# Expert gates: one-hot rows built per token in f16, members spread over ten pairs, gates from pair 21

## The chip, the cores and the metric

The kernel runs on one core of a Trainium2 chip. The metric is device microseconds (us) from launch to the end of that core. The kernel before takes 1699.96 us, the median of three runs (1698.5 to 1701.6).

## The reference, cut to what matters

Two transformer-like blocks run over 256 tokens of width 1024. The change lies in the last layer of the second block, a layer of 16384 experts (128 x 128). Each of 8 heads picks 16 experts for a token, and their softmax gives 16 gates.

```python
s = jnp.einsum('thpd,hpnd->thpn', q, sub_keys)
sc, idx = lax.top_k(s, PEER_TOPK)
cand = (sc[:, :, 0, :, None] + sc[:, :, 1, None, :]).reshape(T, PEER_HEADS, PEER_TOPK * PEER_TOPK)
cidx = (idx[:, :, 0, :, None] * PEER_NKEYS + idx[:, :, 1, None, :]).reshape(...)
top_sc, pos = lax.top_k(cand, PEER_TOPK)
eidx = jnp.take_along_axis(cidx, pos, axis=-1)
gate = jax.nn.softmax(top_sc.astype(jnp.float32), axis=-1).astype(h.dtype)
act = jax.nn.gelu(jnp.einsum('thkd,td->thk', u_tab[eb], hb), approximate=False)
y = jnp.einsum('thk,thkd->td', gb * act, v_tab[eb])
```

## The kernel before, in words

All of the change is in `experts(hx)`. The kernel does not gather the chosen experts. It computes the activations of all 16384 for all tokens, multiplies them by a gate that is zero for those not chosen, and sums over all.

The loop `for m in range(KEYS // 2)` runs over 64 pairs of weight tiles (128 experts a tile). For each tile, `weights` loads 512 KB (`wraw`), ScalarE rounds it to a high part (`whi`, L99), VectorE or GpSimd subtracts that from the raw tile to get the low part (`wlo`, L100: GpSimd below pair 11, VectorE from there), and TensorE does 24 matmuls of 256 columns (`mm3`, L119 to L121: high by high, high by low, low by high, so that the third matmul of a tile is the first that needs `wlo`). There are three buffers of each of `wraw`, `whi` and `wlo`. ScalarE applies Gelu to a pair's result (L1370, L1372).

Beside the first pairs, VectorE chooses the experts. `choosing` is a generator whose steps the table `pace` deals out, so many before each pair: two steps of `keys_of`, four of `pairs` for each half of the tokens, and then `members`, which finds the two key numbers of every chosen expert: eight steps, four for each half of the tokens, in turn one of two VectorE instructions over 2048 elements (L1267, L1270) and one of a reduction over 2048 (L1272). Some of them are kept in program order. The rest is placed by a scheduler, within each engine's own queue.

At pair `DIRECT`, `softmaxes` makes two tables: `tab` (the two key numbers) and `gtab` (the gate in two f16 parts), with the chosen expert on the partition and the token along the row. From then on `gates(t4, n)` is called `PACE` times a pair on average, 64 times in all, for four tokens at a time. It builds one-hot rows: `oij` (is this row's key number equal to the column's number, for both key numbers), and `og` (the second one-hot times the gate, in two parts). Eight matmuls of 128 columns (L1326) multiply them to the 128 x 128 table of gates of each of the four tokens, and the result is multiplied into the activations by VectorE (L1329) or laid down ahead for the pairs to come by ScalarE (L1331). The tiles `oij` and `og` have two buffers each.

After the last pair, a second loop of 128 tiles sums the weighted rows (L1396); its first matmul waits for all gates.

Of the kernel before, what the change touches and what calls it, by code (L numbers as in the profile page):

```python
# [13 lines left out]
F16 = mybir.dt.float16  # L14
U32 = mybir.dt.uint32
AF = mybir.ActivationFunctionType
ALU = mybir.AluOpType
# [29 lines left out]
def two_blocks(ctx: ExitStack, tc: tile.TileContext, A, out):  # L47
    nc = tc.nc
    act, vec, pool, pe = nc.scalar, nc.vector, nc.gpsimd, nc.tensor
# [34 lines left out]
    def bank(name):  # L84
        ids = banks[-1][name]
        ids.append(ids.pop(0))
        return ps.tile([128, 512], F32, name=name, tag=f"bank{ids[-1]}")
# [96 lines left out]
    with psum(mm=8):  # L184
        o = bank("mm")
# [6 lines left out]
    for k in range(KC):  # L192
        if k % 4 < 2:
            first[k % 4] = next(loads[k % 4])
        t = hp.tile([128, T1], F32, name=f"h{k}")
# [932 lines left out]
    def experts(hx):  # L1128
        NEGL = -3.0e38

        GATE = 2.0 ** 14
        DIRECT = 18
        PACE = 1.5
        es = ExitStack()
        early = ExitStack()
        early.enter_context(psum(mm=6, sc=2))
# [11 lines left out]
        for i in range(2):  # L1148
            for e2 in range(2):
                o = bank("sc")  # L1150
                for k in range(4):
                    pe.transpose(o[:, k * 128:(k + 1) * 128], hx[4 * e2 + k][:, i * 128:(i + 1) * 128], ident)
                t = qp.tile([128, 2, S], F32, name="pair").rearrange("p a b -> p (a b)")
# [7 lines left out]
        for n in range(6):  # L1161
            o = bank("mm")
            project(o[:, :S + 2], wt(A["peer_wq"][n], vec if n == 1 else pool), raw, t1=S + 2)
            rp.append(o)
            if n == 0:
                o = bank("sc")
# [9 lines left out]
        p = es.enter_context(tc.tile_pool(name="ex", bufs=1))  # L1176
        iota = p.tile([128, 128], F32, name="iota")
        nc.sync.dma_start(out=iota, in_=A["iota"])
        acts = p.tile([128, KEYS, S], F32, name="acts")

        tab = p.tile([128, 2, S], F32, name="tab")
        gtab = p.tile([128, 2, S], F32, name="gtab")
# [92 lines left out]
        def expert_acts(m, e, pin):  # L1275

            o = bank("mm")
            for e2 in range(2):
                hi, lo = wt(A["peer_u"][2 * m + e2], e, pin=pin)
                for k in range(KC):  # L1280
                    c = slice(k * 128, (k + 1) * 128)
                    mm3(o[:, e2 * S:(e2 + 1) * S], hi[:, c], lo[:, c], u3[k][0], u3[k][1], k == 0, k == KC - 1)
            return o.rearrange("p (a b) -> p a b", a=2)
# [26 lines left out]
        def gates(t4, n):  # L1310

            o = bank("sc")
            ts = slice(4 * t4, 4 * t4 + 4)
            oij = pg.tile([128, 2, 4, 128], F16, name="oij")
            og = pg.tile([128, 2, 4, 128], F16, name="og")
            vec.tensor_tensor(out=oij, in0=iota[:, None, None, :].to_broadcast([128, 2, 4, 128]),  # L1316
                              in1=tab[:, :, ts][:, :, :, None].to_broadcast([128, 2, 4, 128]), op=ALU.is_equal)
            for part in range(2):
                if part and t4 % 2:
                    vec.tensor_mul(og[:, 1], oij[:, 1], gtab[:, 1, ts][:, :, None].to_broadcast([128, 4, 128]))  # L1320
                else:
                    for k in range(4):
                        act.activation(og[:, part, k], oij[:, 1, k], AF.Copy, scale=gtab[:, part, 4 * t4 + k:4 * t4 + k + 1])  # L1323
            for k in range(4):
                for part in range(2):
                    pe.matmul(o[:, k * 128:(k + 1) * 128], lhsT=og[:, part, k], rhs=oij[:, 0, k], start=part == 0, stop=part == 1)  # L1326
            gv = o.rearrange("p (n i) -> p i n", n=4)
            av = acts[:, :, ts]
            vec.tensor_mul(av[:, :n], av[:, :n], gv[:, :n])  # L1329
            if n < KEYS:  # L1330
                act.copy(av[:, n:], gv[:, n:])  # L1331
# [8 lines left out]
        def choosing():  # L1340

            for q in range(NH - 2, NH):
                yield from keys_of(q)
            for i in range(2):
                yield from pairs(i)
            for i in range(2):
                yield from members(i)
# [1 line left out]


        steps = choosing()
        pace = (1, 1, 1, 2, 1, 1, 1, 2, 1, 1, 0) + (1, 1, 1, 1, 1, 1, 0)
        OTHER = 11
        done = 0
        for m in range(KEYS // 2):
            if m < DIRECT:
                for n in range(pace[m]):
                    next(steps)
            if m == DIRECT:
                for _ in steps:  # L1360
                    pass
                softmaxes()
                et.close()
                eg = ExitStack()
                pg = eg.enter_context(tc.tile_pool(name="exg", bufs=2))
            o = expert_acts(m, pool if m < OTHER else vec, OTHER <= m < DIRECT)
            a = acts[:, 2 * m:2 * m + 2]
            if done:
                t = qp.tile([128, 2, S], F32, name="pair")
                act.activation(t[:, :, :done], o[:, :, :done], AF.Gelu)  # L1370
            if done < S:
                act.activation(a[:, :, done:], o[:, :, done:], AF.Gelu)  # L1372
            if done:
                vec.tensor_mul(a[:, :, :done], a[:, :, :done], t[:, :, :done])
            if m >= DIRECT:
                for _ in range(int((m - DIRECT + 1) * PACE) - int((m - DIRECT) * PACE)):
                    if done < S:
                        gates(done // 4, 2 * m + 2)
                        done += 4
# [28 lines left out]
        part = acts[:, 16:24].rearrange("p (i a) b -> p i (a b)", i=4)  # L1408
# [4 lines left out]
        for i in range(2):  # L1413
            for n in range(3):
                add(ws[n], i, False, n == 2)
            for e2 in range(2):
                fs = slice(e2 * 512, (e2 + 1) * 512)
                t, x = part[:, 2 * i + e2], hf[:, i, fs]
# [23 lines left out]
    gated_mix()  # L1442
    stages.close()
    experts(hx)


# [133 lines left out]
```

## Time and profile before

| what | value |
|---|---|
| runs, median of three | 1699.96 us |
| profiled execution, its own time | 1698.82 us |
| its span on the core | 1697.0 us |
| mean granted TensorE clock | 0.992 |
| PE busy | 1659.4 us, 98% |
| VectorE (DVE) busy | 1298.1 us, 76% |
| ScalarE (ACT) busy | 1011.0 us, 60% |

The span runs from the first to the last instruction of the core, and 1.8 us of the execution's own time lie around it. Busy shares are means over the whole span. Matmuls overlap, so a duration of 0.28 us in a row is longer than the distance from one start to the next, about 0.12 us for 256 columns. The same holds to a smaller degree on VectorE: an instruction starts about 0.08 us before the end of the one ahead of it. What an instruction costs its engine is the distance from its start to the next one's, which is called its pitch below.

### The profile page before, as it was taken

What the parts mean: (1) busy time and instruction counts of PE and PEld (TensorE: products, weight loads), DVE (VectorE), ACT (ScalarE), POOL (GpSimd) and SP (SyncE); (2) the same over time, 40 slices, a digit from 0 to 9 for tenths busy, and PEclk for the clock granted to TensorE, in tenths of its full rate; (3) what the DMA queues carried; (4) which work ended last, traced back from release to release, by engine and by line L of the source; (5) the groups of instructions that cost most, each with busy time, mean ns of one, the idle gap of its engine ahead of it and who ended that gap; (6) DMA issues with size and microseconds to landing.
All of it is one profiled execution on the core that took longest, in us unless ns stands there. A gap on an engine that the chain in (4) does not pass through costs nothing.

```text
span 1697.0 us, 31058 instructions
## 1 busy us (share of the span) xinstructions
PE 1659.4 (98%) x11813; PEld 1537.4 (91%) x11813; DVE 1298.1 (76%) x2356; ACT 1011.0 (60%) x2021; POOL 210.7 (12%) x141
## 2 busy tenths in 40 slices
PE   9999989999999999999999989999999999999997
PEld 8999977799999888889999989999999988888886
DVE  8877767679875788887988997788889656666565
ACT  6444455655553676754664436988888555555554
POOL 3001366230000000000036920000000000000000
PEclk9999999999999999999999989999999999999999
DMA  7877642158786444435545545454444665556553
GB/s 257 289 235 251 207 141 97 38 187 271 253 266 186 157 137 138 149 107 196 184 154 182 175 139 171 160 165 165 165 165 163 200 227 197 193 192 197 190 196 124
DMA packets 90486, 308.21 MB, mean 182 GB/s; under 512 B 11352, under 2 KB 13912, under 8 KB 90208
## 3 DMA queue, kind: packets, MB, share of 16 engines
q1 hardware_dynamic: 90336, 306.22, 54.8%
q8 instruction: 93, 1.52, 0.4%
q14 instruction: 57, 0.47, 0.1%
HBM read 304.08 MB, written 2.10 MB: 180 GB/s over the span
## 4 chain that ended last, share of the span: by engine, by line
PE 64%; DVE 8%; ACT 3%; DMA 2%; issue 1%; DVEq 0%; ACTq 0%; SPq 0%
PE y L1396 20%; PE mm L119 12%; PE mm L121 12%; PE mm L120 11%; PE mm L813 5%; PE sc L1326 2%; DMA wraw<-in_w_in_dram 1%; DVE wlo L100 1%; ACT whi L99 1%; ACT tap L858 1%; DVE xl L744 1%; PE lev L967 1%; DVE acts L1241 1%; DVE acts L1239 0%; DVE acts L1238 0%
## 5 line engine op out<-in xcount | busy, mean ns | idle before, releaser
L99 ACT CAST whi<-wraw 128x1024 fp32r<-128x1024 f32 (+2 forms) x494 | 503.9, 1024 | 346.2 <-PE mm L120 237.3
L100 DVE TENSOR_TENSOR wlo<-wraw,whi 128x1024 fp32r<-128x1024 f32 (+2 forms) x440 | 530.7, 1210 | 195.1 <-ACT whi L99 192.6
L119 PE MATMUL mm<-xh,whi 128*128 128x256 f32 (+1 forms) x2188 | 632.0, 289 | 6.5 <-DVE fk L339 4.6
L121 PE MATMUL mm<-xh,wlo 128*128 128x256 f32 (+1 forms) x2188 | 623.6, 285 | 11.7 <-DVE wlo L100 11.7
L120 PE MATMUL mm<-xl,whi 128*128 128x256 f32 (+1 forms) x2188 | 619.7, 283 | 2.8 <-DVE xl L170 1.6
L121 PEld LDWEIGHTS mm<-xh,wlo 128*128 128x128 f32 x2188 | 414.6, 190 | 13.1 <-DVE wlo L100 13.0
L119 PEld LDWEIGHTS mm<-xh,whi 128*128 128x128 f32 x2188 | 416.0, 190 | 10.5 <-DVE fk L339 4.8
L120 PEld LDWEIGHTS mm<-xl,whi 128*128 128x128 f32 x2188 | 416.3, 190 | 4.7 <-DVE xl L170 2.6
L100 POOL TENSOR_TENSOR wlo<-wraw,whi 128x1024 fp32r<-128x1024 f32 x54 | 133.1, 2472 | 363.7 <-ACT whi L99 363.3
L1396 PE MATMUL y<-wlo,gah 128*128 128x512 f32 x512 | 158.0, 389 | 0.0
L1396 PE MATMUL y<-whi,gah 128*128 128x512 f32 x512 | 158.0, 389 | 0.0
L1396 PE MATMUL y<-whi,gal 128*128 128x512 f32 x512 | 157.6, 389 | 0.0
L177 ACT CAST gah<-acts 128x256 fp32r<-128x256 f32 x128 | 52.0, 408 | 149.7 <-PE y L1396 149.7
L1323 ACT ACTIVATE og<-oij,gtab 128x128 f16<-128x128 f16 x384 | 123.8, 394 | 18.4 <-DVE oij L1316 18.2
L813 PE MATMUL mm<-xw,wraw 128*128 128x256 f32 x560 | 131.2, 381 | 0.0
L1396 PEld LDWEIGHTS y<-wlo,gah 128*128 128x128 f32 x512 | 96.1, 188 | 20.3 <-DVE wlo L100 0.4
L1396 PEld LDWEIGHTS y<-whi,gah 128*128 128x128 f32 x512 | 96.1, 188 | 20.3 <-ACT pair L1370 0.3
L1396 PEld LDWEIGHTS y<-whi,gal 128*128 128x128 f32 x512 | 96.1, 188 | 19.9
L813 PEld LDWEIGHTS mm<-xw,wraw 128*128 128x128 f32 x560 | 101.9, 190 | 13.1 <-issue 0.4
L178 DVE TENSOR_TENSOR gal<-acts,gah 128x256 fp32r<-128x256 f32 x128 | 54.3, 425 | 59.6 <-PE y L1396 59.6
L1316 DVE TENSOR_TENSOR oij<-iota,tab 128x1024 f16<-128x1024 f32 x64 | 77.8, 1221 | 1.7 <-PE sc L1326 1.6
L722 DVE CUSTOM_DVE_ANT_0 ada_w<-ada_w,silu_c 128x1024 f32<-128x1024 f32 x48 | 58.4, 1219 | 0.5 <-DMA ada_w<-in_ada_w_dram 0.5
(904 smaller groups left out, 2395.8 us busy)
## 6 DMA issues: line engine op xcount, KB each, us to landing
wraw<-in_peer_u_dram SPq DMA_DIRECT2D x128, 512.0 KB, 3.3
wraw<-in_peer_v_dram SPq DMA_DIRECT2D x125, 512.0 KB, 4.3
wraw<-in_w_gu_dram SPq DMA_DIRECT2D x80, 512.0 KB, 4.5
wraw<-in_w_in_dram SPq DMA_DIRECT2D x80, 512.0 KB, 3.3
ada_w<-in_ada_w_dram SPq DMA_DIRECT2D x48, 512.0 KB, 4.9
wraw<-in_w_d_dram SPq DMA_DIRECT2D x32, 512.0 KB, 4.3
wraw<-in_w_out_dram SPq DMA_DIRECT2D x16, 512.0 KB, 3.2
wraw<-in_peer_wq_dram SPq DMA_DIRECT2D x16, 512.0 KB, 3.3
```

The lines of the kernel that those rows point to most:

```text
L99: act.copy(hi[:, c], raw[:, c])
L100: sub = (e or vec).tensor_sub(lo[:, c], raw[:, c], hi[:, c])
L119: pe.matmul(o, lhsT=wh, rhs=xh, start=first, stop=False)
L120: pe.matmul(o, lhsT=wh, rhs=xl, start=False, stop=False)
L121: pe.matmul(o, lhsT=wl, rhs=xh, start=False, stop=last)
L177: act.copy(hi, x)
L178: vec.tensor_sub(lo, x, hi)
L722: tc.keep_in_program_order(vec.tensor_tensor_reduce(w, w, row, 1.0, 0.0, op0=ALU.mult, op1=ALU.add, accum_out=ada[:, g:g + 1]))
L813: pe.matmul(o, lhsT=w[:, k * 128:(k + 1) * 128], rhs=xw[k], start=k == 0, stop=k == KC - 1)
L1316: vec.tensor_tensor(out=oij, in0=iota[:, None, None, :].to_broadcast([128, 2, 4, 128]), in1=tab[:, :, ts][:, :, :, None].to_broadcast([128 ...
L1323: act.activation(og[:, part, k], oij[:, 1, k], AF.Copy, scale=gtab[:, part, 4 * t4 + k:4 * t4 + k + 1])
L1396: pe.matmul(y[i][e2], lhsT=x[:, ts], rhs=v[:, e2 * 512:(e2 + 1) * 512], start=first and n == 0, stop=last and n == 2)
```

## The change

A copy of the row of numbers 0 to 127 in f16 (`iota16`) is made once. `gates` now issues twelve small VectorE instructions where it issued one or two large ones and four or eight on ScalarE. For each of four tokens it makes one comparison of `iota16` with the first key number, and, for each of the two parts, one comparison with the second key number followed by the multiplication by the gate. Key number and gate are operands of one value a partition, called pointer operands below. Before, both came as rows spread by a stride of zero. `og` is now written by VectorE alone. The steps of `members` are dealt to pairs 11 to 20 instead of 8, 9 and 11 to 16, the gates begin at pair 21 instead of 18, and 1.55 instead of 1.5 calls are made a pair.

```diff
-        DIRECT = 18
-        PACE = 1.5
+        DIRECT = 21
+        PACE = 1.55
...
+        iota16 = p.tile([128, 128], F16, name="iota16")
+        act.copy(iota16, iota)
...
-            oij = pg.tile([128, 2, 4, 128], F16, name="oij")
+            oi = pg.tile([128, 4, 128], F16, name="oi")
             og = pg.tile([128, 2, 4, 128], F16, name="og")
-            vec.tensor_tensor(out=oij, in0=iota[:, None, None, :].to_broadcast([128, 2, 4, 128]),
-                              in1=tab[:, :, ts][:, :, :, None].to_broadcast([128, 2, 4, 128]), op=ALU.is_equal)
-            for part in range(2):
-                if part and t4 % 2:
-                    vec.tensor_mul(og[:, 1], oij[:, 1], gtab[:, 1, ts][:, :, None].to_broadcast([128, 4, 128]))
-                else:
-                    for k in range(4):
-                        act.activation(og[:, part, k], oij[:, 1, k], AF.Copy, scale=gtab[:, part, 4 * t4 + k:4 * t4 + k + 1])
+            for k in range(4):
+                t = 4 * t4 + k
+                vec.tensor_scalar(oi[:, k], iota16, tab[:, 0, t:t + 1], None, op0=ALU.is_equal)
+                for part in range(2):
+                    vec.tensor_scalar(og[:, part, k], iota16, tab[:, 1, t:t + 1], gtab[:, part, t:t + 1], op0=ALU.is_equal, op1=ALU.mult)
             for k in range(4):
                 for part in range(2):
-                    pe.matmul(o[:, k * 128:(k + 1) * 128], lhsT=og[:, part, k], rhs=oij[:, 0, k], start=part == 0, stop=part == 1)
+                    pe.matmul(o[:, k * 128:(k + 1) * 128], lhsT=og[:, part, k], rhs=oi[:, k], start=part == 0, stop=part == 1)
...
-        pace = (1, 1, 1, 2, 1, 1, 1, 2, 1, 1, 0) + (1, 1, 1, 1, 1, 1, 0)
+        pace = (1, 1, 1, 2, 1, 1, 1, 2, 0, 0, 0) + (1, 1, 1, 0, 1, 1, 1, 0, 1, 1)
```

Line numbers behind the gates shift by one or two: L1329 becomes L1328, L1374 becomes L1373, L1267, L1270 and L1272 become L1269, L1272 and L1274.

The first place is VectorE's queue where pair 11 begins and the first `wlo` tiles of VectorE stand (in peer_u's loop). Before:

```order
L1267 TENSOR_TENSOR acts<-acts,iota 128x2048
L1291 TENSOR_TENSOR eg_10689<-eg_10689,gs_12497 128x128
L1270 TENSOR_TENSOR acts<-acts 128x2048
L1272 TENSOR_REDUCE ei_10684<-acts 128x128
L1267 TENSOR_TENSOR acts<-acts,iota 128x2048
L1270 TENSOR_TENSOR acts<-acts 128x2048
L100 TENSOR_TENSOR wlo<-wraw,whi 128x1024 x2
L1272 TENSOR_REDUCE ej_10685<-acts 128x128
L100 TENSOR_TENSOR wlo<-wraw,whi 128x1024 x2
L1267 TENSOR_TENSOR acts<-acts,iota 128x2048
```

And now, in the same place:

```order
L1269 TENSOR_TENSOR acts<-acts,iota 128x2048
L1293 TENSOR_TENSOR eg_10691<-eg_10691,gs_12685 128x128
L1272 TENSOR_TENSOR acts<-acts 128x2048
L100 TENSOR_TENSOR wlo<-wraw,whi 128x1024 x2
L1274 TENSOR_REDUCE ei_10686<-acts 128x128
L100 TENSOR_TENSOR wlo<-wraw,whi 128x1024 x2
L1269 TENSOR_TENSOR acts<-acts,iota 128x2048
L1272 TENSOR_TENSOR acts<-acts 128x2048
L100 TENSOR_TENSOR wlo<-wraw,whi 128x1024 x4
L1274 TENSOR_REDUCE ej_10687<-acts 128x128
```

The first two `wlo` tiles stand behind two instructions of 2048 elements now instead of five, and later steps have two or four `wlo` tiles between them.

The second place is VectorE's queue at the first calls of `gates`. Before (pairs 18 to 20):

```order
L100 TENSOR_TENSOR wlo<-wraw,whi 128x1024
L1306 TENSOR_TENSOR gtab<-gtab 128x128
L1316 TENSOR_TENSOR oij<-iota,tab 128x1024 x2
L100 TENSOR_TENSOR wlo<-wraw,whi 128x1024
L1320 TENSOR_TENSOR og<-oij,gtab 128x512
L1329 TENSOR_TENSOR acts<-acts,sc 128x38x4
L1316 TENSOR_TENSOR oij<-iota,tab 128x1024
L1374 TENSOR_TENSOR acts<-acts,pair 128x2x4
```

And now (pairs 21 to 23), where the sequence of the second to fifth row goes on until 36 small instructions have been issued, with two L1328 and one L1373 among them, and then the last two rows stand:

```order
L100 TENSOR_TENSOR wlo<-wraw,whi 128x1024
L1308 TENSOR_TENSOR gtab<-gtab 128x128
L1320 TENSOR_SCALAR oi<-iota_10675,tab 128x128
L1322 TENSOR_SCALAR og<-iota_10675,tab,gtab 128x128 x2
L1320 TENSOR_SCALAR oi<-iota_10675,tab 128x128
...
L100 TENSOR_TENSOR wlo<-wraw,whi 128x1024
L1328 TENSOR_TENSOR acts<-acts,sc 128x46x4
```

Between the two `wlo` tiles of pair 23 stand the whole of three calls of `gates` now; before, two comparisons stood between the two tiles of pair 20.

The third place is ScalarE's queue where the scores of the keys are copied, before the expert loop. Now:

```order
L777 ACTIVATE pair<-pair,rc 128x256 x2
L1235 COPY acts<-sc 128x256 x2
L1180 CAST iota_10675<-iota 128x128
L99 CAST whi<-wraw 128x1024
L1222 COPY pair<-mm 128x256
```

The row of L1180 is new there, and a tile's `whi` stands behind it. It waits for the load of `iota`.

## Rows read from the trace of the kernel before

**Rows 1.** The page's part 1: busy time of each engine.
```profile
PE 1659.4 (98%) x11813; PEld 1537.4 (91%) x11813; DVE 1298.1 (76%) x2356; ACT 1011.0 (60%) x2021; POOL 210.7 (12%) x141
```

**Rows 2.** Stretches of the expert stage: us, busy of each engine, TensorE clock.
```profile
core 0: us, PE busy (x) PEld busy (x) DVE busy (x) ACT busy (x) POOL busy (x), PEclk, DMA share, GB/s
937.00:984.00 47.00, 47.00 (x400) 47.00 (x399) 47.00 (x141) 21.98 (x26) 42.58 (x18) 1.00 0.55 185
999.60:1003.00 3.40, 3.40 (x16) 3.40 (x17) 3.40 (x3) 0.00 (x0) 0.00 (x0) 0.50 0.71 180
1056.00:1325.00 269.00, 268.13 (x2502) 265.50 (x2502) 228.31 (x282) 232.62 (x607) 0.00 (x0) 1.00 0.50 164
1338.70:1687.60 348.90, 348.86 (x1538) 287.96 (x1536) 211.37 (x262) 187.25 (x262) 0.00 (x0) 1.00 0.59 193
```

**Rows 3.** Waits of PE from 937 to 1050 us: total, times, longest.
```profile
PE mm L121 <- DVE wlo L100: 9.8, 2, 8.3
```

**Rows 4.** Groups by line, PE from 1056 to 1325 us, idle last.
```profile
L121 PE MATMUL mm<-xh,wlo 128*128 128x256 f32 x665 | 187.7, 282 | 0.7 <-DVE wlo L100 0.7
```

**Rows 5.** Timeline of PE and of VectorE around pair 11: start, us.
```profile
991.04 0.28 PE L120 MATMUL mm<-xl,whi 128*128 128x256 f32 x1
999.60 0.58 PE L121 MATMUL mm<-xh,wlo 128*128 128x256 f32 x1 [8.28 <-DVE wlo L100]
...
986.08 0.21 DVE L1260 TENSOR_SCALAR acts<-acts 128x128 uint32<-128x128 uint32 x1
986.22 0.21 DVE L1261 TENSOR_SCALAR acts<-acts 128x128 uint32<-128x128 uint32 x1
...
989.16 2.28 DVE L1270 TENSOR_TENSOR acts<-acts 128x2048 f32<-128x2048 f32 x1
991.47 2.29 DVE L1272 TENSOR_REDUCE ei<-acts 128x128 f32<-128x2048 f32 x1
...
998.33 2.35 DVE L100 TENSOR_TENSOR wlo<-wraw,whi 128x1024 fp32r<-128x1024 f32 x2
```

**Rows 6.** Timeline of ScalarE and VectorE where the gates begin.
```profile
1038.12 0.59 ACT L1372 ACTIVATE acts<-mm 128x512 f32<-128x512 f32 x1
1043.80 0.59 ACT L1372 ACTIVATE acts<-mm 128x512 f32<-128x512 f32 x1
...
1051.90 2.35 DVE L1316 TENSOR_TENSOR oij<-iota,tab 128x1024 f16<-128x1024 f32 x2
```

**Rows 7.** Groups by line, VectorE from 1056 to 1325 us: busy, mean ns.
```profile
L100 DVE TENSOR_TENSOR wlo<-wraw,whi 128x1024 fp32r<-128x1024 f32 x83 | 101.1, 1223 | 34.6 <-ACT whi L99 34.2
L1329 DVE TENSOR_TENSOR acts<-acts,sc 128x152 f32<-128x152 f32 (+31 forms) x64 | 29.2, 482 | 1.7 <-PE sc L1326 1.7
L1374 DVE TENSOR_TENSOR acts<-acts,pair 128x8 f32<-128x8 f32 (+41 forms) x42 | 17.6, 420 | 2.1 <-ACT pair L1370 2.0
```

**Rows 8.** Timeline of VectorE among the gates: one start to the next.
```profile
1112.09 0.69 DVE L1320 TENSOR_TENSOR og<-oij,gtab 128x512 f16<-128x512 f16 x1
1112.69 1.22 DVE L100 TENSOR_TENSOR wlo<-wraw,whi 128x1024 fp32r<-128x1024 f32 x1
1113.83 1.23 DVE L1316 TENSOR_TENSOR oij<-iota,tab 128x1024 f16<-128x1024 f32 x1
1114.97 1.22 DVE L100 TENSOR_TENSOR wlo<-wraw,whi 128x1024 fp32r<-128x1024 f32 x1
```

**Rows 9.** Timeline of VectorE in the attention, small instructions back to back.
```profile
287.40 0.15 DVE L548 RECIPROCAL sums<-sums 128x2 f32<-128x2 f32 x1
287.47 0.42 DVE L616 TENSOR_TENSOR fvT<-mm,rstd 128x272 f32<-128x272 f32 x1
287.81 0.55 DVE L551 TENSOR_SCALAR P<-P,sums 128x144 f32<-128x144 f32 x2
288.28 0.36 DVE L545 CUSTOM_DVE_ANT_0 P<-sc,masks,rq_ti 128x144 f32<-128x144 f32 x1
...
304.63 0.55 DVE L526 TENSOR_SCALAR decay<-sum,rfq_t,cum_t 128x272 f32<-128x272 f32 x1
305.10 0.41 DVE L178 TENSOR_TENSOR o1l<-po,o1h 128x256 fp32r<-128x256 f32 x1
```

**Rows 10.** The load of `iota`, and ScalarE's next `whi`.
```profile
L1178 SPq DMA_DIRECT2D iota<-in_iota_dram x1: 373/373/373, 893.3 to 893.3; - x1
DMA to landing us min/median/max: 3.0/3.0/3.0
...
897.39 1.05 ACT L99 CAST whi<-wraw 128x1024 fp32r<-128x1024 f32 x1 [1.91 <-PE mm L120]
```

## The prediction

> **What bounds the kernel now.** I began with the page's busy times: PE is busy for 1659.4 us and VectorE for 1298.1 us [rows 1]. These are shares of the whole span, so I cut the expert stage into stretches [rows 2]. The reader is to see that PE is busy for 268.1 of 269 us while the gates are made (1056 to 1325 us) and for all of the second loop (1338.7 to 1687.6 us). VectorE is busy for 228 of the 269 us, ScalarE for 233. So PE sets the end of the gate stretch, with VectorE at 85% behind it, and nothing that is taken off ScalarE there gains more than the 0.7 us that PE waits in it [rows 4].
>
> Then I asked for PE's waits before the gates. There are two, 9.8 us together, both for `wlo` from VectorE, the longer 8.3 us [rows 3]. The timeline shows where it comes from: PE needs the first `wlo` of pair 11 at 991.04 and gets on at 999.60, since VectorE works through five long instructions of `members` and makes `wlo` only at 998.33 [rows 5]. After that PE's clock is granted at 0.50, the lower of its two levels: 16 matmuls in 3.4 us, 0.21 us each instead of 0.12 [rows 2]. VectorE, then, is where a gain or a loss must come from.
>
> **The members, spread.** Two long instructions now stand ahead of the first `wlo` of pair 11, the second of which ends at VectorE's 991.47 [rows 5]. So `wlo` starts at 991.5 instead of 998.3, and PE goes on at about 992.7 instead of 999.6: 6.9 us won. The wait that is left is about 1.6 us; the lower level of the clock cost some 16 x 0.09 = 1.5 us, which goes too if so short a wait does not bring it on. The second wait (9.8 - 8.3 = 1.5 us) and the 0.7 us at the gates' start may go as well. From that I take off about a microsecond for new short waits, since a step of two long instructions with two `wlo` behind it (2 x 2.3 + 2 x 1.14 = 6.9 us) is longer than a pair on PE (5.68 us between two Gelus [rows 6]); the pairs without a step make up for it. Net about 10 us, if PE sets the end of the gate stretch: the second loop would begin at 1328.7 instead of 1338.7.
>
> **The gates, price of one call.** Before, a call costs VectorE one L1316 (1.14 us from its start to the next one's) and every other time one L1320 (0.60 us) [rows 8]: 1.44 us on average. Now it is four instructions with one pointer operand and eight with two, over 128 f16 elements. The trace has no such instruction, so I build the price up.
>
> - An instruction of almost no elements takes 0.07 us: L548, 287.40 to 287.47 [rows 9]. 128 four-byte elements without a pointer take 0.14 us (L1260, 986.08 to 986.22 [rows 5]). So 128 such elements cost about 0.065 us.
> - With one pointer: the two L551 (144 and 272 f32 elements) take 287.81 to 288.28, 0.47 us. 416 elements are 0.21 us of that, which leaves 0.13 us for each instruction [rows 9].
> - With two pointers: L526 over 272 elements takes 0.47 us (304.63 to 305.10), L616 over 272 without a pointer 0.34 us (287.47 to 287.81) [rows 9]. Both read PSUM. The difference, 0.13 us, is for two pointers: 0.07 + 0.13 = 0.20, or 0.19 if I count the 0.06 us of L551 twice.
> - The f16 elements: bounds are nothing and 0.065 us (the four-byte rate). No row is near either end, and I take the middle, 0.03 us, as half the bytes.
>
> That gives 0.16 and 0.22 us, and 4 x 0.16 + 8 x 0.22 = 2.40 us a call. The upper bound is 4 x 0.195 + 8 x 0.26 = 2.86 us. The lower bound is twelve instructions at the price without a pointer, 12 x 0.14 = 1.7 us.
>
> [...]
>
> **The sum on VectorE.** In the kernel before the first comparison starts 8.1 us after the Gelu of the pair ahead of the gates (1043.80 to 1051.90 [rows 6]); that chain (Exp, tables, transposes) is the same now. Pair 11 goes on at 992.7, so the Gelu of pair 20 starts near 992.7 + 10 x 5.68 + 1 = 1050.5, and the gates at 1058.6. From there VectorE has: 81 tiles of `wlo` at 1.14 us (92.3; the last of pair 23 and those of 24 to 63); 64 L1328 at 0.42 us (26.9: mean 0.482 less the 0.08 us that an instruction's end lies under the next, plus 0.02 as the gates come three pairs later and cover more rows); 42 L1373 at 0.34 us (14.3) [rows 7, 8]. Together 133.5 us, and 64 calls at 2.40 us: 153.6. VectorE's last `wlo` is then done at 1058.6 + 287.1 = 1345.7, and PE's last 24 matmuls take another 2.8 us: 1348.5 against 1338.7 before, 9.8 us later. PE alone would be through at 1328.7. So VectorE becomes the bound of the gate stretch, and its excess eats the 10 us of the members and as much again. Waits of VectorE itself add perhaps 1 us: L1328 waits for PE's gate matmuls, and behind it in the queue stand the rest of the comparisons and the next `wlo`, for which PE waits in turn.
>
> **Costed at nothing.** The f16 copy of `iota` waits on ScalarE for a load that is issued at 893.3 and lands 3.0 us later. Behind it stands a `whi` that PE's matmuls held until 897.39 anyway [rows 10]; without that cover the wait would be at most a microsecond. ScalarE loses its `og` work, and PE hardly waited for it [rows 4]. Gate matmuls on PE are the same number. The gates now end at pair 62 instead of 60, one pair before the second loop; that loop has VectorE at 211 of 349 us [rows 2] and stays as it is.
>
> **How the numbers follow.** The profiled execution took 1698.8 us; plus 9.8 and about 1 is 1709.6. The median of the runs is 1.1 us above that execution, which is within their own spread. I predict 1710 us. A measurement of this kernel can tell about 0.2% (3.4 us) from no change.
>
> **Rivals.**
> - *A pointer costs little behind a pointer* (faster, chance 0.28). The place is the same twelve instructions. If the mean price is under 0.174 us (2.09 us a call: (1328.7 - 2.8 - 1058.6 - 133.5) / 64), VectorE stays ahead and PE sets the end: 10 us less, 1689. For it: no row shows two such instructions with two pointers back to back, and the second pointer rests on one form that reads PSUM; with it free, 12 x 0.16 = 1.92 us. Against: one pointer adds 0.06 us in the L551 rows, and two add 0.13 us in the L526 row [rows 9]. [...]
> - *The price lies at the tie* (no change, 0.12): 0.175 to 0.2 us, that is 2.1 to 2.3 us a call, gives 1697 to 1703. At 2.25 us both effects cancel.
> - *f16 runs no faster than four-byte elements* (slower, 0.14): at 2.86 us a call the second loop starts 64 x 0.46 = 29 us later again, near 1739.
> - *The members still hold PE up* (0.03): if the wait stays at 8 us, for a load or a reduction, VectorE's gates begin that much later too: 1717.
> - The forecast itself, VectorE-bound between 1703.4 and 1726: 0.43.
>
> So faster 0.28, same 0.12, slower 0.60. The range from 1687 (PE-bound, with a microsecond over) to 1725 leaves out the case near 1739 and a little more, under 0.2. The forecast's own range is 1704 to 1718.
>
> **What would show it.** Right: PE waits for `wlo` all through the gate stretch, some 20 us in sum; VectorE is busy for over 95% of it, with ScalarE near half; a comparison with one pointer starts 0.16 us before the next instruction and one with two pointers 0.22 us; the wait at pair 11 falls from 8.3 to under 2 us, and with it the stretch at half clock. Wrong: pitches near 0.1 us with PE at 99% would make it the first rival; pitches of 0.26 us and more, the third; a long wait at pair 11 would show that the order of the members was not what held it.

## The result, and the profile after

The changed kernel takes 1721.16 us (median of four runs, 1718.59 to 1722.77) against 1699.62: a ratio of 1.0128, 95% interval 1.0113 to 1.0144. It is slower, as forecast and by the mechanism that was forecast, but by 21.5 us and not by 10. The profiled execution is the fastest of the four, 1718.59 us, so its trace shows 19.8 of the 21.5 us.

The page of the changed kernel, part 1 (compare [rows 1]):

```profile
PE 1670.3 (97%) x11813; PEld 1538.7 (90%) x11813; DVE 1357.8 (79%) x3025; ACT 904.6 (53%) x1637; POOL 210.6 (12%) x141
```

Its gate stretch, a part of it at the lower clock, and the second loop (compare [rows 2]):

```profile
core 0: us, PE busy (x) PEld busy (x) DVE busy (x) ACT busy (x) POOL busy (x), PEclk, DMA share, GB/s
1060.00:1345.00 285.00, 270.75 (x2400) 258.50 (x2399) 280.97 (x931) 122.78 (x220) 0.00 (x0) 0.99 0.44 145
1330.60:1334.00 3.40, 3.40 (x19) 3.40 (x18) 3.40 (x14) 0.12 (x1) 0.00 (x0) 0.51 0.78 230
1357.00:1707.00 350.00, 348.94 (x1538) 287.97 (x1536) 212.08 (x263) 187.31 (x262) 0.00 (x0) 1.00 0.57 193
```

VectorE is busy for 281 of 285 us now, PE for 271, ScalarE for 123. The bound has moved from PE to VectorE. The second loop begins at 1357.0 instead of 1338.7.

PE's waits from 937 to 1060 us (compare [rows 3]), and then from 1059 to 1360 us (compare [rows 4]):

```profile
PE mm L121 <- DVE wlo L100: 1.9, 2, 1.3
```

```profile
PE mm L121 <- DVE wlo L100: 10.9, 23, 0.9
PE mm L119 <- ACT whi L99: 2.3, 3, 0.9
PE y L1395 <- ACT pair L1369: 1.1, 1, 1.1
PE sc L1325 <- DVE og L1322: 0.5, 3, 0.2
```

The long wait of 8.3 us at pair 11 is down to 1.3 us, and in its place PE waits 23 times, up to 0.9 us, all through the gates.

VectorE's queue at pair 11 (compare [rows 5]) and a piece of the gates, by start and duration:

```profile
989.01 2.28 DVE L1272 TENSOR_TENSOR acts<-acts 128x2048 f32<-128x2048 f32 x1
991.21 2.35 DVE L100 TENSOR_TENSOR wlo<-wraw,whi 128x1024 fp32r<-128x1024 f32 x2
...
1102.24 0.25 DVE L1320 TENSOR_SCALAR oi<-iota,tab 128x128 f16<-128x128 f16 x1
1102.41 0.53 DVE L1322 TENSOR_SCALAR og<-iota,tab,gtab 128x128 f16<-128x128 f16 x2
1102.85 0.25 DVE L1320 TENSOR_SCALAR oi<-iota,tab 128x128 f16<-128x128 f16 x1
```

The first `wlo` starts at 991.2 (forecast 991.5). An instruction with one pointer takes 1102.24 to 1102.41, and two with two pointers take 1102.41 to 1102.85, 0.22 each.

### The profile page after: what moved, and what is told of

Same layout as the page of the kernel before. It is cut to its first block, busy times and chain, and to the rows that moved or that the text cites. A ratio compares the mean times of both kernels' runs of the same rounds, so it can differ in the third digit from the quotient of the medians.

```text
span 1716.5 us, 31287 instructions
## 1 busy us (share of the span) xinstructions
PE 1670.3 (97%) x11813; PEld 1538.7 (90%) x11813; DVE 1357.8 (79%) x3025; ACT 904.6 (53%) x1637; POOL 210.6 (12%) x141
## 4 chain that ended last, share of the span: by engine, by line
PE 52%; DVE 17%; ACT 4%; DMA 3%; issue 2%; DVEq 0%; ACTq 0%; SPq 0%
PE y L1395 20%; PE mm L121 8%; PE mm L120 8%; PE mm L119 8%; PE mm L813 5%; DVE og L1322 4%; DVE wlo L100 4%; DMA wraw<-in_peer_u_dram 2%; DVE oi L1320 2%; ACT whi L99 1%; DMA wraw<-in_w_in_dram 1%; DVE acts L1328 1%; ACT tap L858 1%; DVE xl L744 1%; PE lev L967 1%
## 5 line engine op out<-in xcount | busy, mean ns | idle before, releaser
L1322 DVE TENSOR_SCALAR og<-iota,tab,gtab 128x128 f16<-128x128 f16 x512 | 136.2, 306 | 0.0
L1395 PEld LDWEIGHTS y<-whi,gah 128*128 128x128 f32 x512 | 96.1, 188 | 21.5 <-ACT pair L1369 1.5
L1320 DVE TENSOR_SCALAR oi<-iota,tab 128x128 f16<-128x128 f16 x256 | 62.9, 246 | 0.0
```

Source lines behind the costliest of these rows:

```text
L1320: vec.tensor_scalar(oi[:, k], iota16, tab[:, 0, t:t + 1], None, op0=ALU.is_equal)
L1322: vec.tensor_scalar(og[:, part, k], iota16, tab[:, 1, t:t + 1], gtab[:, part, t:t + 1], op0=ALU.is_equal, op1=ALU.mult)
L1395: pe.matmul(y[i][e2], lhsT=x[:, ts], rhs=v[:, e2 * 512:(e2 + 1) * 512], start=first and n == 0, stop=last and n == 2)
```

## The experiments

The theory was that VectorE's sum from the first call of `gates` to its last `wlo` sets the end, at 0.16 and 0.22 us an instruction. Times are compared with the kernel before on the same chip (1697.8 us for the first four runs below, 1698.0 for the one with the doubled gate matmuls, 1698.8 for the others).

**The members alone.** The kernel before with three numbers changed.

```diff
-        DIRECT = 18
-        PACE = 1.5
+        DIRECT = 21
+        PACE = 1.55
-        pace = (1, 1, 1, 2, 1, 1, 1, 2, 1, 1, 0) + (1, 1, 1, 1, 1, 1, 0)
+        pace = (1, 1, 1, 2, 1, 1, 1, 2, 0, 0, 0) + (1, 1, 1, 0, 1, 1, 1, 0, 1, 1)
```

> Only the spread of the members and the later, slightly denser gates (from pair 21, 1.55 a pair); a call of gates builds its rows as in the kernel before. Theory (VectorE's sum is the bound of the changed kernel, 0.163 and 0.223 us an instruction): a call costs VectorE 1.44 us, so PE sets the end; the wait at pair 11 is near 1.6 us, no stretch at half clock behind it, and the second loop starts near 1329: 1688 to 1691 us. Rival (the spread of the members, or the shorter stretch for the gates, costs time by itself): 1700 or more.

Measured: 1689.75 us, ratio 0.9951 (0.9933 to 0.9968). PE's waits from 937 to 1060 us:

```profile
PE mm L121 <- DVE wlo L100: 1.3, 1, 1.3
```

The gate stretch of the same kernel:

```profile
1060.00:1325.00 265.00, 263.74 (x2462) 260.32 (x2461) 228.17 (x281) 231.43 (x611) 0.00 (x0) 1.00 0.47 162
```

This half of the change is a gain of 0.5%, the 10 us of the forecast less two, and PE stays the bound. Of the versions that leave nothing out it has the lowest median.

**The gates alone.** The changed kernel with the old `pace`, `DIRECT` and `PACE` (the diff above, read backwards).

> Only the new way to build the rows; members and gates are dealt out as in the kernel before (gates from pair 18, 1.5 a pair). Theory (VectorE's sum from the first call to its last wlo decides): the gates start 7 us earlier at 1052 but VectorE has 6 more wlo tiles (6.8 us) from there, so the time is that of the changed kernel within 3 us: 1717 to 1724. Rival (the two parts add up, so that without the spread of the members their 10 us are missing): 1729 to 1733.

Measured: 1721.61 us, ratio 1.0143 (1.0124 to 1.0163). The long wait at pair 11 is back, and yet the second loop begins at 1357.1, where it does in the changed kernel. PE's waits from 937 to 1060 us:

```profile
PE mm L121 <- DVE wlo L100: 8.6, 2, 8.3
```

So the two halves do not add up: once VectorE is the bound, what PE wins before the gates is lost, and the whole loss comes from the gates. That the second loop begins at the same tenth of a microsecond is partly chance: the gates begin at 1048.3 here, not at the 1052 that was expected, and behind PE's last wait for `wlo`, at 1334.2, PE runs on without a wait and sets the end itself. The gate stretch of this kernel has no part at half clock:

```profile
1060.00:1345.00 285.00, 273.96 (x2457) 263.64 (x2456) 280.89 (x909) 126.71 (x224) 0.00 (x0) 1.00 0.46 154
```

**One part of the gates built, used twice.** The gate's second part is left out and the first is used in its place; PE does the same number of matmuls.

```diff
-                for part in range(2):
+                for part in range(1):
                     vec.tensor_scalar(og[:, part, k], ...)
...
-                    pe.matmul(o[...], lhsT=og[:, part, k], ...)
+                    pe.matmul(o[...], lhsT=og[:, 0, k], ...)
```

> The changed kernel, but the gate's second part is not built: the matmuls use the first part twice, so PE's work is the same and the output is not the reference's. A call costs VectorE 4 x 0.163 + 4 x 0.223 = 1.54 us instead of 2.44. Theory: that is under the 2.09 us at which PE takes over, so PE sets the end: 1688 to 1692 us. Rival (what holds PE is the hand-over of the rows to the gate matmuls with two buffers, or the small instructions as such, not VectorE's sum): over 1703 us.

Measured: 1688.24 us, ratio 0.9939 (0.9919 to 0.9958). Its gate stretch:

```profile
1060.00:1325.00 265.00, 265.00 (x2487) 262.89 (x2486) 238.02 (x701) 128.19 (x229) 0.00 (x0) 1.00 0.49 164
```

PE is busy for 265.0 of 265 us. Eight small instructions a call and the hand-over with two buffers hold up nothing; the sum does.

**Pointers counted.** The first one-hot compares with a constant, one part multiplies by a constant, the other keeps two pointers. The rows built are then no longer those of the chosen experts.

```diff
-                vec.tensor_scalar(oi[:, k], iota16, tab[:, 0, t:t + 1], None, op0=ALU.is_equal)
+                vec.tensor_scalar(oi[:, k], iota16, 5.0, None, op0=ALU.is_equal)
...
+                vec.tensor_scalar(og[:, 0, k], iota16, tab[:, 1, t:t + 1], 0.25, ...)
+                vec.tensor_scalar(og[:, 1, k], iota16, tab[:, 1, t:t + 1], gtab[:, 1, t:t + 1], ...)
```

> The changed kernel, but with fewer pointer operands: the first one-hot compares with a constant (no pointer), the first part of the second multiplies by a constant (one pointer), the second part keeps its two pointers. The output is not the reference's. Theory (0.06 us for each pointer on top of 0.07 us and 0.03 us for the elements): pitches 0.10, 0.16 and 0.22 us in one trace, 4 x (0.10 + 0.16 + 0.22) = 1.94 us a call, under the 2.09 us at which PE takes over: 1688 to 1692 us. Rival (the price lies in the comparison in f16 and not in the pointers): all three near 0.2 us and a time near the changed kernel's.

Measured: 1689.57 us, ratio 0.9955 (0.994 to 0.9969). VectorE's timeline, where L1320 has no pointer, L1321 one and L1322 two:

```profile
1153.94 0.18 DVE L1320 TENSOR_SCALAR oi<-iota 128x128 f16<-128x128 f16 x1
1154.04 0.24 DVE L1321 TENSOR_SCALAR og<-iota,tab 128x128 f16<-128x128 f16 x1
1154.21 0.31 DVE L1322 TENSOR_SCALAR og<-iota,tab,gtab 128x128 f16<-128x128 f16 x1
1154.43 0.19 DVE L1320 TENSOR_SCALAR oi<-iota 128x128 f16<-128x128 f16 x1
```

From start to start 0.10, 0.17 and 0.22 us: each pointer adds 0.06 us here, the second as much as the first. The second operation (the multiplication) adds nothing that the rows show: L1321 with it and one pointer takes the 0.17 us that L1320 of the changed kernel takes with one pointer and the comparison alone (1102.24 to 1102.41). With eight pointers of twenty taken out and twelve left, PE is the bound again.

**One instruction of twelve less.** For one token of four the second part is left out, and the first is used in its place.

```diff
-                for part in range(2):
+                for part in range(2 if k else 1):
...
-                    pe.matmul(o[...], lhsT=og[:, part, k], ...)
+                    pe.matmul(o[...], lhsT=og[:, part if k else 0, k], ...)
```

> The changed kernel, but for one token of the four in a call the gate's second part is not built (the matmul takes the first twice; the output is not the reference's, PE's work is the same): one two-pointer instruction less a call, 2.22 us instead of 2.45. Theory (above 2.09 us a call the time goes with VectorE's sum): 64 x 0.22 = 14 us less than the changed kernel, 1705 to 1709 us, with waits of PE for wlo that are left. Rival (a step: either all of the loss or none, since waits come in whole tiles): near 1689 or above 1714.

Measured: 1700.2 us, ratio 1.0013 (1.0003 to 1.0022). VectorE is still the bound, as the theory has it, with PE at 264 of 270 us:

```profile
1060.00:1330.00 270.00, 264.46 (x2418) 257.49 (x2418) 268.59 (x874) 123.34 (x223) 0.00 (x0) 1.00 0.47 155
```

But the time fell by 21 us for 14 us of VectorE's work, and both the theory's interval and its rival missed it. In the two profiled executions the second loop begins at 1338.3 here and at 1357.0 in the changed kernel, 18.7 us apart. VectorE's rows from the first comparison to its last `wlo` of the pairs account for that: 15.6 us more of instructions, 2.6 us more of waits and gates that begin 1.1 us later, less 0.6 us from there to the second loop. The stretch above was granted the full clock throughout, so the clock is no part of what this kernel loses. PE's waits for `wlo` from 1060 to 1340 us are fewer than in the changed kernel:

```profile
PE mm L121 <- DVE wlo L100: 4.2, 9, 0.9
```

**Numbers in f32.** The other direction, with nothing left out: by the estimate of 0.065 us for 128 four-byte elements and half of it for f16, 12 x 0.033 us more a call.

```diff
-                vec.tensor_scalar(oi[:, k], iota16, ...)
+                vec.tensor_scalar(oi[:, k], iota, ...)
-                    vec.tensor_scalar(og[:, part, k], iota16, ...)
+                    vec.tensor_scalar(og[:, part, k], iota, ...)
```

> The changed kernel, but the row of numbers that the twelve instructions read is the f32 one; they still write f16. This is the third rival's price. Theory: 0.195 and 0.255 us instead of 0.163 and 0.223, 12 x 0.033 = 0.4 us a call more, 64 x 0.4 = 25 us later: 1741 to 1750 us. Rival (the elements' type does not matter, a pointer's fixed price hides it): the changed kernel's time within 5 us.

Measured: 1762.52 us, ratio 1.0379 (1.0355 to 1.0402). That is 41 us above the changed kernel, where the sum gave 25. The stretch from 1060 to 1400 us:

```profile
1060.00:1400.00 340.00, 303.78 (x2494) 286.94 (x2493) 318.44 (x957) 128.47 (x230) 0.00 (x0) 0.93 0.38 127
```

What PE waits for most from 1060 to 1395 us (sum, count, longest):

```profile
PE mm L121 <- DVE wlo L100: 25.3, 25, 2.7
```

What VectorE waits for most from 1060 to 1402 us:

```profile
DVE acts L1373 <- ACT pair L1369: 17.7, 15, 1.7
```

The mean clock is 0.93: the trace has 11 stretches at half clock there, 44 us in sum. And VectorE, the bound, is itself idle for over 20 us, mostly at L1373, which needs a pair's Gelu and so PE to be through with the pair. PE is late there not for want of speed on the whole, but behind the stretches at half clock. One of them, and VectorE's wait behind it:

```profile
1140.20:1143.60 3.40, 3.18 (x15) 3.18 (x16) 3.40 (x11) 0.37 (x1) 0.00 (x0) 0.50 0.59 183
1148.76 0.30 DVE L1373 TENSOR_TENSOR acts<-acts,pair 128x136 f32<-128x136 f32 x1 [1.33 <-ACT pair L1369]
```

Of VectorE's 12 waits of more than 0.9 us at L1373, 11 end 4 to 11 us after one of the 11 stretches began.

**The same, with PE kept busier.** Is the half clock a cause or a sign? On top of the f32 numbers, each gate matmul is issued twice, the second over the first.

```diff
-            for k in range(4):
+            for k in [n for k in range(4) for n in (k, k)]:
                 for part in range(2):
                     pe.matmul(o[...], lhsT=og[:, part, k], ...)
```

> The kernel with the f32 row of numbers (1762.5 us, 44 us of its gate stretch at half clock), but each pair of gate matmuls is issued twice, the second time over the first: 512 matmuls of 0.055 us more, 28 us of work for PE and nothing more for any other engine. It tests whether the half clock is a cause or only a sign of PE's waits. Theory C (PE's waits bring the clock down, and a PE at half clock then makes VectorE wait, 22 us in that run; a busier PE keeps its clock): the half clock in the gate stretch falls below 20 us, VectorE waits less, and the time falls by 5 to 15 us in spite of the added work: 1747 to 1757 us. Rival (the half clock costs nothing, since VectorE is late anyway, and the added matmuls lie in PE's waits or add to the path): 1762 us or more.

Measured: 1748.4 us, ratio 1.0295 (1.0278 to 1.0312). With 28 us more work on PE the kernel is 14 us faster. The same stretch:

```profile
1060.00:1400.00 340.00, 326.38 (x3072) 310.45 (x3071) 326.26 (x969) 136.80 (x243) 0.00 (x0) 0.98 0.41 136
```

What VectorE waits for most from 1060 to 1402 us:

```profile
DVE acts L1373 <- ACT pair L1369: 7.3, 6, 2.2
```

The clock is 0.98 (10 us at half clock instead of 44), VectorE waits 10 us less at L1373, and the time is the changed kernel's plus 27 us, about what the sum alone asks for (25). A rival is the order of the queue, since the scheduler placed some of the L1373 a few instructions earlier or later here. But five of the long waits of the f32 kernel are at an L1373 that stands in the same place in both queues, and there VectorE waited 7.3 us in sum before and 0.6 us now. The one shown above at 1148.76, with its wait of 1.33 us, is now:

```profile
1142.97 0.28 DVE L1373 TENSOR_TENSOR acts<-acts,pair 128x136 f32<-128x136 f32 x1
```

So in these two runs the half clock is a cause: PE waits for VectorE's `wlo` (25.3 us in the f32 run, 9.4 with the doubled matmuls), is granted half its clock (44 us and 10), falls behind, and then VectorE waits for PE (17.7 us and 7.3 at L1373). It is not the only one: two waits of 1.8 and 1.9 us that are left have no such stretch ahead of them.

**Two ways to help VectorE with GpSimd.** First, pair 11's `wlo` by GpSimd too, on top of the members alone:

```diff
-        OTHER = 11
+        OTHER = 12
```

> Only the spread members with the old gates, and GpSimd makes wlo for pair 11 too (OTHER 12 instead of 11). Theory: VectorE then has a pair's time (5.7 us) more before its first wlo, so the wait of 1.3 us at pair 11 goes: 1 to 2 us less than the members alone, 1686 to 1690 us. Rival: VectorE's instructions beside GpSimd's two tiles get longer (a comparison of 128 elements took 2.42 us beside one in the kernel before, 0.21 us alone) and the wait only moves to pair 12: 1689 to 1692.

Measured: 1692.77 us, ratio 0.9965 (0.9951 to 0.9979), no better than without it. VectorE's timeline, and GpSimd's behind it:

```profile
988.05 4.48 DVE L1267 TENSOR_TENSOR acts<-acts,iota 128x2048 f32<-128x2048 f32 x1
```

```profile
987.80 2.58 POOL L100 TENSOR_TENSOR wlo<-wraw,whi 128x1024 fp32r<-128x1024 f32 x1 [0.45 <-ACT whi L99]
990.64 4.14 POOL L100 TENSOR_TENSOR wlo<-wraw,whi 128x1024 fp32r<-128x1024 f32 x1 [0.26 <-ACT whi L99]
```

VectorE's instruction and GpSimd's second tile take 4.48 and 4.14 us instead of their usual 2.3 and 2.4. They end one after the other: VectorE's ends 2.2 us after GpSimd's first tile (990.38), and GpSimd's second tile 2.3 us after VectorE's instruction (992.53). The wait moves to the next pair (2.3 us there, 3.2 in all). The rival was right in its mechanism, and its interval (1689 to 1692) was missed by 0.8 us.

Second, every second `wlo` of the changed kernel's gate stretch by GpSimd:

```diff
-            hi, lo = wt(A["peer_u"][2 * m + e2], e, pin=pin)
+            hi, lo = wt(A["peer_u"][2 * m + e2], pool if m > DIRECT and e2 else e, pin=pin)
```

> The changed kernel, with wlo of every second tile from pair 22 on made by GpSimd (2.4 us each) instead of VectorE: VectorE's sum is 42 x 1.14 = 48 us shorter. Theory A (VectorE's sum alone): PE sets the end, 1688 to 1692 us. Theory B (a one-source instruction of VectorE that runs while GpSimd works waits for it to end, as one of 128 elements took 2.42 us beside GpSimd in the kernel before): the small instructions stand still for a good part of 42 x 2.4 = 101 us, more than the 48 us saved, 1735 us or more. I hold B.

Measured: 1753.26 us, ratio 1.0325 (1.031 to 1.0341). VectorE's timeline, and GpSimd's at the same time behind it:

```profile
1155.38 1.23 DVE L100 TENSOR_TENSOR wlo<-wraw,whi 128x1024 fp32r<-128x1024 f32 x1
1156.51 2.40 DVE L1320 TENSOR_SCALAR oi<-iota,tab 128x128 f16<-128x128 f16 x1
1158.83 0.53 DVE L1322 TENSOR_SCALAR og<-iota,tab,gtab 128x128 f16<-128x128 f16 x2
```

```profile
1155.76 3.09 POOL L100 TENSOR_TENSOR wlo<-wraw,whi 128x1024 fp32r<-128x1024 f32 x1 [3.54 <-ACT whi L99]
```

A comparison of 0.25 us takes 2.40, until GpSimd's tile, which started 0.75 us before it, ends at 1158.85. From 1060 to 1390 us the L1320 last 0.43 us in the mean and the L1322 0.38, where they last 0.25 and 0.31 in the changed kernel. Over 251 and 503 of them that is some 84 us more, against the 48 us of `wlo` that GpSimd takes over: it took no work off VectorE on balance here, and the time is 32 us above the changed kernel's.

## Why the prediction was right or wrong

*The members.* Right. The wait at pair 11 fell to 1.3 us (forecast 1.6), the clock was granted in full behind it up to 1330.6, and alone the spread gives 8 us (forecast 10).

*The price of a call.* Right to 2%. Some 0.164 and 0.224 us against 0.16 and 0.22: a call takes 2.45 us instead of 2.40, 3.3 us over 64 calls, which is a third of the 10 us that were forecast. The pointers cost what the attention's rows said, and the count of pointers confirmed that each is paid for (0.06 us). The first rival (a second pointer for nothing) fell with it. The third (no gain from f16) did not happen; its prices of 0.195 and 0.26 us ask for 25 to 29 us more over 64 calls, and with f32 put in and PE kept busier the time was 27 us above the changed kernel's.

*The bound.* Right. The gates begin at 1059.1 (forecast 1058.6), VectorE is busy for 98.6% of the stretch, and the runs put the price at which PE takes over between 1.94 us a call (PE sets the end, 1690 us) and 2.22 (VectorE does, 1700 us), on either side of the 2.09 of the sum. One sign was missed: PE's waits for `wlo` sum to 10.9 us, not to some 20. By an estimate from PE's rows a wait also costs about 0.26 us that counts as busy: the matmul ahead of it is listed for 0.28 us instead of being followed after 0.12, and the one behind it is followed after 0.22 (as from 1329.99 to 1330.21).

*The size: wrong by half.* The mechanism held, and terms of the sum were too small. The step that failed is the end of it, "Waits of VectorE itself add perhaps 1 us" together with PE's tail of 2.8 us, and beside it the price above. I let VectorE's work run on as one block that waits for nobody, and I took PE to be as far as VectorE when VectorE's last `wlo` is done. The second loop starts at 1357.0, 8.5 us after the 1348.5 of the sum, to which that 1 us was still to be added. VectorE's rows give these 8.5 us. The gates begin 0.5 us later. The price adds 3.3 us. Between the gates' start and the end of VectorE's last `wlo` of the pairs, at 1352.2, VectorE waits 4.0 us, against about 1. PE begins the second loop 4.8 us after that `wlo`, not 2.8: it has 40 matmuls left by then and not 24. The other terms are 1.3 us smaller, as 63 L1328 and 40 L1373 stand ahead of that `wlo` and not 64 and 42. What VectorE waits for from 1059 to 1352 us, without its shortest waits:

```profile
DVE acts L1373 <- ACT pair L1369: 2.7, 6, 1.1
DVE acts L1328 <- PE sc L1325: 0.6, 2, 0.4
DVE wlo L100 <- ACT whi L99: 0.3, 1, 0.3
```

The longest of them stands behind the stretch at half clock (1330.6 to 1334.0), in which a matmul starts every 0.21 us instead of every 0.12:

```profile
1338.72 0.66 DVE L1373 TENSOR_TENSOR acts<-acts,pair 128x480 f32<-128x480 f32 x1 [1.07 <-ACT pair L1369]
```

The tail is not owed to the clock: PE waits for `wlo` again after that stretch, for the last time at 1345.28, and in the run with one instruction less, with the clock granted in full, PE begins the second loop 5.4 us after VectorE's last `wlo` of the pairs.

Then the second loop is 1.1 us longer, for a wait at its start. The other 1.7 us to the median lie outside this execution and are left open; the other executions' granted clock is one to three thousandths lower, which would fit more half clock but does not show it.

The f32 pair of runs shows what the clock can add: the 25 us of VectorE's work that f32 puts on top by the sum came to 41 us with 44 us at half clock, and to 27 us with PE kept busier and 10 us at half clock. In the changed kernel's profiled execution it adds little: one stretch of 3.4 us with a wait of 1.1 us behind it, and the gates alone take the same time with no such stretch among the gates. How it is in the executions that were not profiled stays open.

## What to carry to other kernels

Price small VectorE instructions by the start-to-start distance of the nearest row, pointer by pointer, and multiply by the count: twelve at 0.2 us replaced work of 1.44 us. When two sums of some 280 us decide, a forecast of their difference needs every small term: 0.05 us a call, a few waits and the matmuls still to do at the end were most of what made 10 us into 21. When VectorE's sum passes PE's own by much, the loss can outgrow the excess, as in the f32 run: a PE that waited was granted half its clock for 44 us and then held up the engine that held it up. Part a change that does two things: here one half gains 8 us and the other loses 24, and the loss hides the gain.

## What the runs showed of the hardware

- Adding 512 redundant matmuls to a kernel whose PE waited made it 14 us faster (1762.5 to 1748.4). No single wait of PE for `wlo` was longer than 2.7 us in the kernel that spent 44 us of its gate stretch at half clock, in 11 stretches (25 waits, 25.3 us in sum). The 23 waits of up to 0.9 us in the changed kernel came with one stretch of 3.4 us, and 9 of up to 0.9 us in the run with one instruction less came with none.
- A VectorE comparison of 128 f16 elements cost 0.10 us with constants in the run that counted pointers, and 0.06 us more for each operand of one value a partition (0.17 and 0.22 us from start to start). A multiplication in the same instruction added nothing (0.17 us with one such operand, with it there and without it in the changed kernel).
- f32 numbers in place of f16, with PE kept busier, cost 27 us over 768 instructions, waits included: 0.035 us for each 128 elements, about half of the 0.065 us that I had estimated for 128 four-byte elements as a whole from L548 (0.07 us) and L1260 (0.14 us).
